# The two parts of the activations get a pool of their own, at a fixed distance from the weight parts

## The chip, the cores and the metric

One of the eight cores of a Trainium2 chip runs the whole program. The metric is the device time of one execution in microseconds, the median of three runs. TensorE (PE) multiplies, VectorE (DVE) and ScalarE (ACT) do everything between the products, SyncE (SP) issues the loads.

## The reference

A two-layer decoder trunk for 256 tokens of width 1024, in float32. Cut to what matters here:

```python
for l in range(DEPTH):                                   # two layers
    h = rmsnorm(x, norm_mix_g[l])
    if l % 2 == 0:
        proj = h @ e_w_in[e]                             # 1024 x 6144
        ya = rg_lru(causal_dwconv(xa), ...) * gelu(ga)
        yb = hgrn2_mix(qb, fb, ib, gb, ...)
        mix = concatenate([ya, yb]) @ e_w_out[e]         # 2048 x 1024
    else:
        proj = h @ o_w_in[o]                             # 1024 x 6176
        mix = mamba2_mix(...) @ o_w_out[o]               # 2048 x 1024
    x = x + mix
    x = x + mem_cross_attn(rmsnorm(x), rmsnorm(mem), xq_w[l], xk_w[l], xv_w[l], xo_w[l])
    hf = rmsnorm(x, norm_ffn_g[l])
    x = x + square(relu(hf @ ffn_w1[l])) @ ffn_w2[l]     # 1024 x 4096 x 1024
return rmsnorm(x, final_norm_g)
```

## The kernel before

All weights stream once from HBM, in an order fixed by `PLAN`, as halves of chunks of 128 x 1024 numbers. For each half SP loads a tile `raw` (line 150), ACT rounds it to float32r as `wh` (line 164), and DVE subtracts to give the rest as `wl` (line 165): two parts whose sum is the float32 weight. The class `Stream` keeps four `raw` buffers and five of each part, splits three halves ahead of the half being multiplied and loads four more ahead of that.

The activations are split in the same way, in tiles of 128 x 2 x 256 numbers (2048 bytes of a partition): `nh` and `nl` (helper `nhl`, four buffers each) after a norm, `yh` and `yl` (helper `yhl`, eight each) for the outputs of the mixers, the heads, the squared ReLU and the memory. A product of two split numbers is three matmuls, high by high, low by high and high by low. There are two kinds:

- `gemm` (lines 451, 453, 454): a 128 x 128 piece of `wh` or `wl` is loaded as the stationary matrix, and 256 columns of an activation part stream through as the moving one.
- `gemm_nat` (lines 470 to 472, and 1151 to 1153 at the very end): a 128 x 128 piece of an activation part is stationary, and 512 columns of weights move.

`chunk` issues them half by half, in the program's order, and between halves `pipe.tick()` lets the short chains of the norms, mixers and heads go on by one step. The scores and outputs of the heads (lines 804 to 806) are split products too, of scratch tiles; the mixers' small products are plain float32.

The tiles of SBUF lie in pools, one behind the other in the order in which these are opened: 16,512 bytes of what the system and its constants need, `cst` (small tables, the residual `xres`), `wp` (`raw`, `wh`, `wl`), `ap` (activations and scratch, each group of buffers behind the one first asked for), then `l0` or `l1`. Tiles are rounded up to 32 bytes. Adding up the sizes: every tile of `wp` begins 64 bytes beyond a multiple of 512, `yh` and `yl` begin 96 bytes beyond one, `nh` and `nl` 384 bytes beyond one. The pieces that matmuls take from them are at whole multiples of 512 bytes from there (`cs` of line 450 steps by 512 bytes, k by 1024), so each product meets the same remainders by 512.

Of the kernel before, what the change touches and what calls it, by code (L numbers as in the profile page):

```python
# [16 lines left out]
P = 128  # L17
# [7 lines left out]

# halves of weight chunks: buffers as loaded and as split, how far ahead they are split, and loaded before that
RAW_BUFS, PART_BUFS, SPLIT_AHEAD, LOAD_AHEAD = 4, 5, 3, 4
# chunks of layer 1's memory keys and values before the groups of the state-space mixer, and with each of them
KV_FIRST, *KV_EACH = 2, 2, 2, 2, 0, 0, 0, 0, 0
# how far short chains are taken ahead of the program's order  # L30
AHEAD = 200

# ---------------------------------------------------------------- the order of the weight chunks
# A chunk is 128 x (kt * cols) with kt * cols = 2048 (or less): kt k-tiles of a block of columns.

# [72 lines left out]

# ---------------------------------------------------------------- columns of the table of small parameters
_FIRST = [("memkv", 16), ("mix", 16)]  # L110
# [15 lines left out]
class Stream:  # L126
    """The halves of the weight chunks in their order: load, and split in two float32r parts."""

# [14 lines left out]
    def loading(self):  # L143
        """the next half, a piece at a time"""
        h = self.loaded
        self.loaded += 1
        hk, n = self._shape(h)
        self.raw[h] = raw = self.pool.tile([P, 1024], F32, tag="raw", bufs=RAW_BUFS, name=f"raw{h // 2}_{h % 2}")
        for a, b in self._pieces(h, hk * n):
            self.nc.sync.dma_start(raw[:, a:b], self.wst[h // 2, h % 2, :, a:b])  # L150
            yield
# [27 lines left out]
    def ahead(self, h):  # L179
        """what goes on while half h is multiplied"""  # L180
        with self.tc.high_priority(offset=0):
            self.split(h + 1 + SPLIT_AHEAD)
            self.load(h + 1 + SPLIT_AHEAD + LOAD_AHEAD)
# [7 lines left out]
class Pipe:  # L191
    """Chains of small steps that are issued a step at a time between the large products."""

# [19 lines left out]
def trunk(ctx: ExitStack, tc: tile.TileContext, wst, small, levels, gatew, xT, memT, fing, out):  # L213
# [3 lines left out]
    cst = ctx.enter_context(tc.tile_pool(name="cst", bufs=1))  # L217
    wp = ctx.enter_context(tc.tile_pool(name="wp", bufs=1))
    ap = ctx.enter_context(tc.tile_pool(name="ap", bufs=1))
    ps = ctx.enter_context(tc.tile_pool(name="ps", bufs=1, space=PSUM))  # L220
# [10 lines left out]
    def sc(i, name, shape=(P, 2, 256)):  # L231
        """scratch, two tiles of 2 KiB for each number"""
        return gt(name, f"s{i}", 2, shape)

    def nhl():
        return gt("nh", "nh", 4, dt=F32R), gt("nl", "nl", 4, dt=F32R)

    def yhl():
        return gt("yh", "yh", 8, dt=F32R), gt("yl", "yl", 8, dt=F32R)

# [29 lines left out]

    # ---------------------------------------------------------------- small helpers
    def seq():
        return tc.manual_schedule(engines={PE.engine})

    def order(after, before, why):
        """two instructions of one engine, in this order"""
        tc.add_manual_dep(after.ins, before.ins.name, NOSYNC, reason=why)
# [19 lines left out]
    def diag(r):  # L297
        """diagonal matrices of the two columns of r, in two parts"""
        dh, dl = (gt(t, t, 2, (P, 2, 128), F32R) for t in ("dgh", "dgl"))
        with tc.high_priority(offset=AHEAD):  # L300
            for j in range(2):
                V.tensor_scalar(dh[:, j, :], ident, r[:, j:j + 1], None, ALU.mult)
            for j in range(2):
                V.scalar_tensor_tensor(dl[:, j, :], ident, r[:, j:j + 1], dh[:, j, :].bitcast(F32),
                                       ALU.mult, ALU.subtract)
        return dh, dl
# [10 lines left out]
    def token_sums(sq, o, fold):  # L317
        """o[:, half] = the sum over channels of sq [channels, 2, tokens]"""
        n = 1 if fold else 2
        if fold:  # L320
            V.tensor_tensor(sq[:, 0, :], sq[:, 0, :], sq[:, 1, :], ALU.add)
        with seq():
            for hf in range(2):
                for c in range(n):
                    PE.matmul(o[:, hf:hf + 1], sq[:, c, 128 * hf:128 * hf + 128], ones[:, :1],  # L325
                              start=(c == 0), stop=(c == n - 1))
# [20 lines left out]
    def gained(hl, src, gain, i0):  # L347
        """src * gain (a column for each of the two tiles) in two parts"""
        h, lo = hl
# [6 lines left out]
    class Norm:  # L356
        """x * gain in two float32r parts, and 1 / rms of every token."""

# [18 lines left out]
        def add(s, xp, p, parts=True):  # L377
            """a chain of steps for one pair of tiles"""
            parts = parts and s.gain is not None
# [33 lines left out]
        def apply(s, xp, p):  # L413
            """the norm applied before the projection"""
            h = sc(3, "hx")
# [9 lines left out]

    # ---------------------------------------------------------------- products with the weights
    def chunk(label, piece, ticks=1, rows=1):
# [14 lines left out]
    def gemm(label, os, H, L, k0=0, first=True, last=True, ticks=1):  # L442
        """os[pair][:, j, :] += W[:, 128 columns of each]^T x over the k-tiles of a chunk"""
        kt = PLAN[st.pos][3]
# [19 lines left out]
    def gemm_nat(label, os, H, L, k0=0, first=True, last=True, ticks=1):  # L464
        """os[half] += x[tokens of the half]^T W over the k-tiles of a chunk, tokens on partitions"""
        kt = PLAN[st.pos][3]
# [8 lines left out]

    # ---------------------------------------------------------------- memory keys and values
    kT, vN = [[], []], [[], []]

    class Memory:
# [13 lines left out]
        def step(s, ticks=1):  # L493
            """the next chunk of the keys, then of the values"""
            i, l, n = s.done, s.l, s.n
# [76 lines left out]

    # ---------------------------------------------------------------- parameters of layer 0's mixers
    def pt():
# [33 lines left out]
    def conv(o, wn, bn, tiles, stride, cv):  # L608
        """width-4 causal depthwise convolution of two tiles"""
        r = sc(cv, "cv")  # L610
# [7 lines left out]

    # ---------------------------------------------------------------- RG-LRU
    def rglru(p, xc, ga):  # L620
# [33 lines left out]

    # ---------------------------------------------------------------- HGRN2
    sts = []
# [8 lines left out]
    def hgrn(p, F, K, q, Q, vg):  # L665
        """scores by halves of blocks of 2, 4, ... 256 tokens; every decay is a product of forget gates"""
        Qf, Kf, Tm = flat(Q), flat(K), flat(F)
# [114 lines left out]

    # ---------------------------------------------------------------- parts that both layers have
    def residual(o, p, nrm):
# [6 lines left out]
    def out_deep(label, H, L, nrm, ticks=1):  # L791
        """x += W^T y, 16 k-tiles in two sweeps over four accumulators"""
        os = [pg() for _ in range(4)]
# [6 lines left out]
    def products(o, pairs):  # L800
        """o = the sum of the products of (stationary, moving), each in two float32r parts"""
        last = len(pairs) - 1
# [5 lines left out]
    def parted(i, name, src):  # L808
        """two float32r parts of src"""
        h, lo = (gt(f"{name}{c}", f"s{i + c}", 2, dt=F32R) for c in range(2))  # L810
# [102 lines left out]

    # ---------------------------------------------------------------- layer 0
    pipe.drain()
# [12 lines left out]

    # ---------------------------------------------------------------- layer 1
    pipe.spawn(m1.prepare())  # L930
# [30 lines left out]
    def steps(o):  # L961
        """dt, and the sums of dt * A within each half of the tokens"""
        with tc.high_priority(offset=AHEAD):
# [30 lines left out]
    def decays(g):  # L994
        """exp(sum over s+1..t of dt A) of four heads, [s, (s0 t0 | s0 t1 | s1 t1)]"""
        E = l1.tile([P, 4, 3, 128], F32, tag="E", bufs=2, name=nm("E"))
# [27 lines left out]
    def ssd(g, E, xs, bc, z):  # L1024
        gap = 3 if g < 7 else 2
        for _ in range(gap):
            yield
        # masked C B^T, and x * dt with tokens on partitions
        cb = pm((P, 512))
# [83 lines left out]

    # ---------------------------------------------------------------- the last sum and norm, with tokens on partitions
    xn = [[sc(4 + 2 * hf + c, "xn", (P, 512)) for c in range(2)] for hf in range(2)]
# [3 lines left out]
    def turn():  # L1119
        """x with tokens on partitions, and the last gain for all of them"""  # L1120
        for c in range(2):
# [61 lines left out]

# ---------------------------------------------------------------- layout on the host

# [65 lines left out]
```

## Time and profile before

| what | value |
|---|---|
| device time, median of 3 runs | 1027.02 us (1026.95 to 1027.9) |
| span of the profiled execution, first to last instruction | 1024.7 us |
| TensorE busy, share of the span | 1012.2 us, 99% |
| VectorE busy | 773.8 us, 76% |
| ScalarE busy | 610.4 us, 60% |
| mean busy share of the DMA engines, and rate | about half, 176 GB/s |
| granted TensorE clock | 0.999 of full speed |

The profiled execution's time is known as its span; the runs are timed on the device as a whole and come out 2.3 us above it. "Busy" of TensorE counts a matmul from its start to its modelled end; consecutive matmuls overlap, so that the share says that TensorE always had one under way, and how fast they follow one another has to be read from their starts.

### The profile page before, as it was taken

What the parts mean: (1) busy time and instruction counts of PE and PEld (TensorE: products, weight loads), DVE (VectorE), ACT (ScalarE), POOL (GpSimd) and SP (SyncE); (2) the same over time, 40 slices, a digit from 0 to 9 for tenths busy, and PEclk for the clock granted to TensorE, in tenths of its full rate; (3) what the DMA queues carried; (4) which work ended last, traced back from release to release, by engine and by line L of the source; (5) the groups of instructions that cost most, each with busy time, mean ns of one, the idle gap of its engine ahead of it and who ended that gap; (6) DMA issues with size and microseconds to landing.
All of it is one profiled execution on the core that took longest, in us unless ns stands there. A gap on an engine that the chain in (4) does not pass through costs nothing.

```text
span 1024.7 us, 20857 instructions
## 1 busy us (share of the span) xinstructions
PE 1012.2 (99%) x8485; PEld 958.2 (94%) x8485; DVE 773.8 (76%) x1471; ACT 610.4 (60%) x886; POOL 1.2 (0%) x6
## 2 busy tenths in 40 slices
PE   8999999999999999999999999999999999999997
PEld 7898988989999999999999999999999999889985
DVE  7968788786887864565699888999989786546653
ACT  6667757674566653464546876778456656535542
POOL 0000000000000000000000000000000000000000
PEclk9999999999999999999999999999999999999999
DMA  8764443444544555555546665444545355555551
GB/s 292 273 218 157 140 150 135 175 146 146 183 145 166 185 185 185 186 187 187 173 150 219 217 189 202 169 162 144 206 135 195 129 166 181 185 185 185 187 184 41
DMA packets 52560, 180.54 MB, mean 176 GB/s; under 512 B 5968, under 2 KB 6128, under 8 KB 52336
## 3 DMA queue, kind: packets, MB, share of 16 engines
q1 hardware_dynamic: 52176, 178.69, 51.8%
q8 instruction: 66, 1.08, 0.4%
q10 hardware_dynamic: 288, 0.52, 0.1%
q14 instruction: 30, 0.25, 0.1%
HBM read 178.11 MB, written 1.08 MB: 175 GB/s over the span
## 4 chain that ended last, share of the span: by engine, by line
PE 90%; DVE 4%; ACT 4%; issue 1%; DMA 1%; SPq 0%; ACTq 0%
PE pg L451 23%; PE pg L453 22%; PE pg L454 22%; PE pg L472 4%; PE pg L470 4%; PE pg L471 4%; DVE wl L165 1%; ACT wh L164 1%; PE pm L325 1%; PE pm L1052 1%; PE pm L804 1%; PE pm L805 1%; PE pm L806 1%; DMA raw<-in_wst_dram 1%; PE pm L675 1%
## 5 line engine op out<-in xcount | busy, mean ns | idle before, releaser
L164 ACT CAST wh<-raw 128x1024 fp32r<-128x1024 f32 (+1 forms) x325 | 336.2, 1038 | 322.9 <-PE pg L453 219.9
L165 DVE TENSOR_TENSOR wl<-raw,wh 128x1024 fp32r<-128x1024 f32 (+1 forms) x325 | 391.4, 1209 | 164.6 <-ACT wh L164 163.9
L451 PE MATMUL pg<-nh,wh 128*128 128x256 f32 x1280 | 362.4, 283 | 0.0
L453 PE MATMUL pg<-nl,wh 128*128 128x256 f32 x1280 | 357.8, 280 | 0.0
L454 PE MATMUL pg<-nh,wl 128*128 128x256 f32 x1280 | 357.1, 279 | 0.0
L451 PEld LDWEIGHTS pg<-nh,wh 128*128 128x128 f32 x1280 | 240.5, 188 | 1.7 <-issue 0.7
L453 PEld LDWEIGHTS pg<-nl,wh 128*128 128x128 f32 x1280 | 240.1, 188 | 0.3
L454 PEld LDWEIGHTS pg<-nh,wl 128*128 128x128 f32 x1280 | 240.1, 188 | 0.0
L451 PE MATMUL pg<-yh,wh 128*128 128x256 f32 x768 | 215.4, 281 | 1.3 <-ACT yh L367 0.7
L453 PE MATMUL pg<-yl,wh 128*128 128x256 f32 x768 | 215.0, 280 | 0.1
L454 PE MATMUL pg<-yh,wl 128*128 128x256 f32 x768 | 214.7, 280 | 0.3 <-DVE wl L165 0.2
L451 PEld LDWEIGHTS pg<-yh,wh 128*128 128x128 f32 x768 | 144.3, 188 | 2.3 <-ACT wh L164 1.3
L454 PEld LDWEIGHTS pg<-yh,wl 128*128 128x128 f32 x768 | 144.2, 188 | 1.0 <-DVE wl L165 0.7
L453 PEld LDWEIGHTS pg<-yl,wh 128*128 128x128 f32 x768 | 144.3, 188 | 0.7 <-DVE yl L374 0.3
L470 PE MATMUL pg<-wh,yh 128*128 128x512 f32 x176 | 69.9, 397 | 0.0
L472 PE MATMUL pg<-wl,yh 128*128 128x512 f32 x176 | 69.6, 396 | 0.0
L471 PE MATMUL pg<-wh,yl 128*128 128x512 f32 x176 | 69.6, 395 | 0.0
L615 DVE SCALAR_TENSOR_TENSOR cv<-pg,smB,cv 128x255 f32<-128x255 f32 (+2 forms) x120 | 49.2, 473 | 0.5 <-ACT cv L612 0.5
L470 PEld LDWEIGHTS pg<-wh,yh 128*128 128x128 f32 x176 | 33.1, 188 | 7.9 <-issue 0.3
L472 PEld LDWEIGHTS pg<-wl,yh 128*128 128x128 f32 x176 | 33.1, 188 | 7.9
L471 PEld LDWEIGHTS pg<-wh,yl 128*128 128x128 f32 x176 | 33.1, 188 | 7.6
L896 DVE SCALAR_TENSOR_TENSOR t<-pg,rb 128x512 f32<-128x512 f32 x32 | 21.9, 690 | 16.5 <-PE pg L454 16.5
(262 smaller groups left out, 1097.5 us busy)
## 6 DMA issues: line engine op xcount, KB each, us to landing
raw<-in_wst_dram SPq DMA_DIRECT2D x317, 512.0 KB, 3.3
ac<-acd SPq DMA_DIRECT2D x16, 256.0 KB, 4.8
mem<-in_memT_dram SPq DMA_DIRECT2D x8, 256.0 KB, 4.4
raw<-in_wst_dram SPq DMA_DIRECT2D x8, 256.0 KB, 4.5
xres<-in_xT_dram SPq DMA_DIRECT2D x4, 256.0 KB, 6.4
gw<-in_gatew_dram SPq DMA_DIRECT2D x1, 1024.0 KB, 7.6
smB<-in_small_dram SPq DMA_DIRECT2D x1, 545.0 KB, 6.9
gn<-in_fing_dram SPq DMA_DIRECT2D x2, 256.0 KB, 3.8
```

The costliest lines, as they stand in the source:

```text
L164: self.last = nc.scalar.copy(hi[:, a:b], raw[:, a:b])
L165: nc.vector.tensor_tensor(lo[:, a:b], raw[:, a:b], hi[:, a:b].bitcast(F32), ALU.subtract)
L325: PE.matmul(o[:, hf:hf + 1], sq[:, c, 128 * hf:128 * hf + 128], ones[:, :1], start=(c == 0), stop=(c == n - 1))
L451: PE.matmul(o[:, j, :], wh[:, cs], xh, start=(first and k == 0 and j == 0), stop=False, skip_group_check=True)
L453: PE.matmul(o[:, j, :], wh[:, cs], xl, start=False, stop=False, skip_group_check=True)
L454: PE.matmul(o[:, j, :], wl[:, cs], xh, start=False, stop=(last and k == kt - 1), skip_group_check=True)
L470: PE.matmul(os[j], h, wh, start=(first and k == 0), stop=False)
L471: PE.matmul(os[j], lo, wh, start=False, stop=False)
L472: PE.matmul(os[j], h, wl, start=False, stop=(last and k == kt - 1))
L615: V.scalar_tensor_tensor(r[:, j, i:], o[:, j, :256 - i], col(wn, (3 - i) * stride + c), r[:, j, i:], ALU.mult, ALU.add)
L675: PE.matmul(tgt[32 * j:32 * j + 32, b // 4, :], Kf[:, 32 * b:32 * b + 32], qq[:, 32 * b:32 * b + 32], start=True, stop=True, tile_position ...
L896: V.scalar_tensor_tensor(t, o, 0.0, b2(n.rb), ALU.max, ALU.mult)
```

## The change

A new pool `mp` is opened between `wp` and `ap`. Its first tile, `shift`, is 112 float32 numbers (448 bytes of a partition) that nobody writes or reads. `nh`, `nl`, `yh` and `yl` now come from this pool with the same shapes, tags and numbers of buffers. Comments and docstrings go; nothing else differs.

```diff
+SHIFT = 112
...
     cst = ctx.enter_context(tc.tile_pool(name="cst", bufs=1))
     wp = ctx.enter_context(tc.tile_pool(name="wp", bufs=1))
+    mp = ctx.enter_context(tc.tile_pool(name="mp", bufs=1))
+    mp.tile([P, SHIFT], F32, name="shift")
     ap = ctx.enter_context(tc.tile_pool(name="ap", bufs=1))
...
+    def part(name, bufs):
+
+        return mp.tile([P, 2, 256], F32R, tag=name, bufs=bufs, name=nm(name))
+
     def nhl():
-        return gt("nh", "nh", 4, dt=F32R), gt("nl", "nl", 4, dt=F32R)
+        return part("nh", 4), part("nl", 4)
 
     def yhl():
-        return gt("yh", "yh", 8, dt=F32R), gt("yl", "yl", 8, dt=F32R)
+        return part("yh", 8), part("yl", 8)
```

By the sizes: `wp` still begins and ends 64 bytes beyond a multiple of 512 (its tiles are multiples of 4096), 448 bytes more make the remainder 0, and with tiles of 2048 bytes all of `nh`, `nl`, `yh`, `yl` begin at whole multiples of 512. The weights then lie 64 bytes beyond the activations, counted by 512, in every product of both kinds. Before, that distance was 480 for `yh` and `yl` (64 less 96) and 192 for `nh` and `nl` (64 less 384). What stays in `ap`, `l0` and `l1` moves back by 64 bytes, counted by 512.

## Rows read from the trace of the kernel before

**Rows 1.** The page: span, and each engine's busy time (share, instructions).

```profile
span 1024.7 us, 20857 instructions
PE 1012.2 (99%) x8485; PEld 958.2 (94%) x8485; DVE 773.8 (76%) x1471; ACT 610.4 (60%) x886; POOL 1.2 (0%) x6
```

**Rows 2.** The page: engines' shares of the chain that ended last.

```profile
PE 90%; DVE 4%; ACT 4%; issue 1%; DMA 1%; SPq 0%; ACTq 0%
```

**Rows 3.** The view of waits: who waited for whom, us in total, times, longest.

```profile
PE pm L523 <- DVE wz L520: 1.2, 1, 1.2
PE pm L675 <- DVE K L711: 1.0, 4, 0.3
...
ACT wh L164 <- PE pg L453: 219.9, 155, 3.4
```

**Rows 4.** Groups by line, TensorE: count after x, then busy us, mean ns.

```profile
L451 PE MATMUL pg<-nh,wh 128*128 128x256 f32 x1280 | 362.4, 283 | 0.0
...
L451 PE MATMUL pg<-yh,wh 128*128 128x256 f32 x768 | 215.4, 281 | 1.3 <-ACT yh L367 0.7 <-ACT wh L164 0.6
...
L470 PE MATMUL pg<-wh,yh 128*128 128x512 f32 x176 | 69.9, 397 | 0.0
...
L470 PE MATMUL pg<-wh,nh 128*128 128x512 f32 x64 | 26.0, 406 | 0.0
...
L804 PE MATMUL pm<-ph,kv 128*128 128x256 f32 x32 | 9.2, 288 | 0.0
...
L1151 PE MATMUL pg<-wh,yh 128*128 128x512 f32 x16 | 6.3, 396 | 0.0
```

**Rows 5.** TensorE by stretches: length, busy us (x matmuls under way in it), granted clock, DMA.

```profile
425.00:465.00 40.00, 40.00 (x342) 1.00 0.57 189
380.00:420.00 40.00, 40.00 (x345) 1.00 0.56 192
562.00:571.00 9.00, 9.00 (x81) 1.00 0.74 237
646.60:654.20 7.60, 7.60 (x69) 1.00 0.75 263
763.20:774.20 11.00, 11.00 (x96) 1.00 0.39 119
885.00:925.00 40.00, 40.00 (x173) 1.00 0.55 185
```

**Rows 6.** Timeline: first and last matmul of three of those stretches; start, duration, us.

```profile
424.81 0.28 PE L454 MATMUL pg<-nh,wl 128*128 128x256 f32 x1
464.98 0.28 PE L453 MATMUL pg<-nl,wh 128*128 128x256 f32 x1
379.77 0.28 PE L451 MATMUL pg<-yh,wh 128*128 128x256 f32 x1
419.90 0.28 PE L454 MATMUL pg<-yh,wl 128*128 128x256 f32 x1
561.82 0.28 PE L453 MATMUL pg<-nl,wh 128*128 128x256 f32 x1
570.89 0.28 PE L451 MATMUL pg<-nh,wh 128*128 128x256 f32 x1
```

**Rows 7.** Timeline: a matmul followed by a pause, between 96.1 and 96.5 us.

```profile
96.11 0.28 PE L453 MATMUL pg<-nl,wh 128*128 128x256 f32 x1
...
96.23 0.28 PE L454 MATMUL pg<-nh,wl 128*128 128x256 f32 x1
96.43 0.35 PEld L675 LDWEIGHTS pm<-Q,K 128*32 128x32 f32 x32
```

**Rows 8.** The chain in order of time: four plain float32 passes of 256 columns.

```profile
72.80 0.86 PE pm L624 x4
```

**Rows 9.** All engines in two stretches of 25 us: PE, PEld, DVE, ACT, POOL busy.

```profile
525.00:550.00 25.00, 24.51 (x204) 24.11 (x205) 24.83 (x47) 13.66 (x19) 0.00 (x0) 1.00 0.57 189
...
725.00:750.00 25.00, 25.00 (x220) 23.89 (x219) 24.40 (x62) 11.03 (x14) 0.00 (x0) 1.00 0.59 210
```

## Prediction before the run

> **What bounds the kernel now.** I read the page's busy times first. TensorE has a matmul under way in 99% of the span, VectorE 76%, ScalarE 60% [rows 1]. "Under way" is not "at its peak", so the chain that ended last comes next: 90% of it are TensorE's matmuls [rows 2]. Then the waits: the longest total wait of a TensorE matmul is 1.2 us, at the very start, and the next is 1.0 us in four pieces, while ScalarE's rounding of weights waits 219.9 us for TensorE to give buffers back [rows 3]. So the splitters and the loads are ahead, and the time is the number of products times the pace at which they follow each other. Nothing in the change alters the number; only the pace can move.
>
> The groups give the numbers [rows 4]. A line of a group stands for one of three matmuls of a split product, so: 3 x 1280 = 3840 products of 256 columns on `nh`/`nl`, 3 x 768 = 2304 on `yh`/`yl`, 3 x (176 + 64 + 16) = 768 of 512 columns with weights moving, and six kinds of 32 = 192 in the heads. Their mean durations (279 to 283 ns and about 396) are latencies and say nothing of the pace. The pace is the distance of starts in a steady stretch. From the first and last start and the count [rows 5, 6]:
>
> - `nh`/`nl`: (464.98 - 424.81) / 341 = 117.8 ns.
> - `yh`/`yl`: (419.90 - 379.77) / 344 = 116.7 ns. A later `yh` stretch has 96 in 11 us, (11.00 + 0.28) / 96 = 117.5 ns, within its resolution the 117.8 of the others.
> - 512 columns: (40.00 + 0.40) / 173 = 233.5 ns, twice that of 256 columns.
> - `nh`/`nl` again, at 562 to 571 us: (570.89 - 561.82) / 80 = 113.4 ns. The stretch at 646.6 to 654.2 us has (7.60 + 0.28) / 69 = 114.2 ns, the same within one product of its count. These are the same buffers as in the first line, at the same remainder by 512.
>
> The sum closes: 3690 x 117.8 + 150 x 113.4 + 2304 x 116.7 + 768 x 233.5 + 192 x 117.8 = 434.7 + 17.0 + 268.9 + 179.3 + 22.6 = 922 us, 90% of the span, as in the chain (150 is 81 + 69). The granted clock is 1.00 in all of these stretches [rows 5], so paces differ for another reason than the clock.
>
> How much room is there? Four passes of 256 columns of plain float32 take 0.86 us, 215 ns each [rows 8]; a split product has the 512-column matmul at 233.5 ns where this row takes 215. If a 256-column product could run at half of it, 107.5 ns, that would be its floor. I call this an estimate from rows 8. The products run 5% to 9% above the floor, and the fast stretch shows that some of that isn't fixed.
>
> **The change, part by part.** *The empty tile* has no instruction: no time. *The pool* has the same tags and buffer numbers, so no wait for a buffer is added and no instruction is moved past another; no DMA is touched. *Scratch* moves by 64 bytes: the heads' 192 products may change their pace by 4.4 ns (117.8 to 113.4), under 0.9 us either way; taken as 0. The plain float32 products I take as unchanged, since they go at the same pass time of 215 ns.
>
> *The remainders* are all that is left. Distance 192 (`nh`) and 480 (`yh`) become 64. No row shows 64, so the pace is bounded. From below: 107.5 ns, the floor. From above: the longest distance of two neighbouring starts that I can read in a steady stretch, 0.12 us [rows 7], so 120 ns for all. Between these I take 113.4 ns, the fastest pace that a row shows for this very sort of product. The reasons: the two groups differ by 1.1 ns at equal clock and equal shape, so layout does enter; `nh`, which begins at a multiple of 64, has reached 113.4, while no stretch of `yh`, which doesn't, is known to; and after the change every activation tile begins as evenly as `nh` and better. Against it: `nh` held 113.4 for only 150 of 3840 products, so even this layout chooses between two paces by how a stretch begins. That is why the chance below is under a half.
>
> - `nh`/`nl`: 3690 x (117.8 - 113.4) = 16.2 us.
> - `yh`/`yl`: 2304 x (116.7 - 113.4) = 7.6 us.
> - 512 columns: weights still move, from the same remainder 64; what was loaded beside them lay at 96 or 384 and comes to lie at 0. Taken as 0; if it followed (233.5 to 226.9, the ratio of 113.4 to 116.7) it would give 768 x 6.6 = 5.1 us more.
>
> What comes late next is VectorE. Twenty-five microseconds at the new pace become 25 x 113.4 / 117.8 = 24.07, and VectorE has 24.83 and 24.40 us of work in the two fullest such stretches [rows 9]: 0.8 + 0.3 = 1.1 us come back. Elsewhere its waits for ScalarE and TensorE are slack.
>
> Sum: 1024.7 - 16.2 - 7.6 + 1.1 = 1002.0 us of span. The median of the runs, 1027.0, is 2.3 us above the profiled span, which I add: 1004.3 us.
>
> [...] A matmul with no weight load beside it shows whether loads and moving reads disturb each other. At 96.23 us a product starts, the next load begins 0.20 us later, when its columns have passed, and yet it takes 0.28 us like the one before it, which had a load beside it [rows 7]; ends are modelled, so this is a hint and no proof. [...]
>
> **The rivals.**
>
> 1. *The change does nothing for the pace.* The stall is the moving stream's own, whatever lies beside it: for it the row at 96.23 us, and that one layout has two paces. Against it the steady 1.1 ns between `nh` and `yh`. Time 1027.0.
> 2. *A small gain:* all 256-column products settle at 116.7 ns, the pace of `yh`. -3690 x 1.1 + 150 x 3.3 = -3.6 us: 1023.4.
> 3. *A small loss, the other side:* with everything aligned like `nh`, everything takes `nh`'s usual pace, 117.8 ns. `yh` loses 2304 x 1.1 = 2.5 us, the fast stretches 150 x 4.4 = 0.7: 1030.2. It decides wherever a stretch fails to fall into the fast pace; `nh` fails in 96% of its products.
> 4. *A larger loss:* at a distance of 64 the moving read, twice as fast, catches up with the weight read just after each start and is held back every time. All at 120 ns: 3690 x 2.2 + 150 x 6.6 + 2304 x 3.3 = 16.7 us: 1043.7. Single distances of 0.12 us speak for it, the steady means of 116.7 to 117.8 against.
> 5. *No stall at all:* 107.5 ns for 256 columns, 3690 x 10.3 + 150 x 5.9 + 2304 x 9.2 = 60.1 us, and with 215 for 512 columns 768 x 18.5 = 14.2 more. VectorE's two stretches give back 25 x 107.5 / 117.8 = 22.8, so 2.0 + 1.6 = 3.6 us. 970.5 without the 512-column part, 956.3 with it.
>
> **How the numbers follow.** The forecast 0.38, rival 1 0.18, 2 0.12, 3 0.15, 4 0.10, 5 0.07. What can be told from no change is 0.2%, 2 us. Faster: 0.38 + 0.12 + 0.07 = 0.57; same: 0.18; slower: 0.15 + 0.10 = 0.25. The range: rivals 1 to 3 and the forecast hold 0.83. Its low end is a pace half way to the floor, 110.45 ns: 3690 x 7.35 + 150 x 2.95 + 2304 x 6.25 = 42.0 us, with 2.4 us back for VectorE 987, and 5.1 less if the 512-column products follow: 982. Its high end is rival 3 with another 0.6 ns on 6144 products: 1034. The forecast's own range, with the same low end and its paces between 110.45 and 114.2, is 982 to 1009.
>
> **What would show it.** In the profile after, the stretches at the same work should have starts 113 to 114 ns apart for both `nh` and `yh`, with no third pace: that is the step that carries 23.8 us. The 512-column stretches should stay at 233.5. Counts of matmuls must be the same, and TensorE's waits a few us at most; VectorE's share rises to 78%. If `nh` stays at 117.8 and `yh` moves towards it, rival 3 is right; if both keep their paces, rival 1. I am wrong outright if the pace goes by how a stretch begins and not by the layout: then no layout holds a fast pace, and the fast stretches only move elsewhere.

## The result and the profile after

| | before | after |
|---|---|---|
| device time, median of 4 runs each | 1027.09 us (1026.95 to 1027.9) | 1010.22 us (1009.63 to 1016.65) |
| ratio | 1 | 0.9849, 95% interval 0.9831 to 0.9868 |
| span of the profiled execution | 1024.7 us | 1008.5 us |
| forecast | | 1004.3 us, range 982 to 1034 |

The change makes the kernel 1.5% faster, 16.9 us, against a forecast of 22.7. The instructions are the same on every engine, in the same order; only line numbers move (the three matmuls of a 256-column split product are now L459, L461 and L462, those of 512 columns L478 to L480).

The page of the changed kernel: span, busy times (share, instructions), shares of the chain that ended last. They answer to [rows 1, 2].

```profile
span 1008.5 us, 20857 instructions
...
PE 994.4 (99%) x8485; PEld 943.2 (94%) x8485; DVE 773.4 (77%) x1471; ACT 610.6 (61%) x886; POOL 1.2 (0%) x6
...
PE 84%; DVE 8%; ACT 4%; issue 1%; DMA 1%; SPq 0%; ACTq 0%
```

TensorE's busy time falls by 17.8 us and the span by 16.2; the work of the other engines is what it was. VectorE's part of the chain doubles from 4% to 8%: of the other engines it grows most. The waits of the changed kernel, against [rows 3] (us in total, times, longest):

```profile
PE pm L683 <- DVE K L719: 1.4, 4, 0.5
PE pm L531 <- DVE wz L528: 1.2, 1, 1.2
...
ACT wh L166 <- PE pg L461: 206.1, 154, 3.4
```

TensorE still waits for almost nothing, so the gain must lie in the pace. TensorE by stretches of one sort of product, against [rows 5] (length, busy us, x matmuls under way, granted clock, DMA share and GB/s):

```profile
245.00:265.00 20.00, 20.00 (x172) 1.00 0.55 187
383.00:415.00 32.00, 32.00 (x285) 1.00 0.57 196
430.00:460.00 30.00, 30.00 (x267) 1.00 0.58 196
526.00:538.00 12.00, 12.00 (x108) 1.00 0.83 254
872.00:912.00 40.00, 40.00 (x176) 1.00 0.58 189
```

By the prediction's rule, (length + one product) / count: `yh` at 383 us goes at (32 + 0.28) / 285 = 113.3 ns (before 116.7), `nh` at 430 us at 30.28 / 267 = 113.4 (before 117.8), `nh` at 526 us at 12.28 / 108 = 113.7, within one product of the same. The 512-column products at 872 us go at 40.39 / 176 = 229.5; first and last start of their 192, 869.98 and 913.69 us, give the better 43.71 / 191 = 228.9 (before, in the same way, 882.81 to 927.36: 233.2). But the first row is `yh` as well, at the same layout and clock, and goes at 20.28 / 172 = 117.9 ns, slower than before. So the changed kernel has two paces.

Over the whole program I take the starts in the trace. In undisturbed stretches of 20 and more there are 5637 products of 256 columns: 4163 of them (74%) follow each other at 113.3 ns, 1474 at 117.8, and the 116.7 of `yh` is gone. Apart from its first few distances, no stretch of them changes its pace before something interrupts it.

The balance of the span, each matmul counted from its start to the next one's: `nh` of 256 columns -11.2 us, `yh` of 256 columns -5.1, 512 columns -2.9; pauses of over 135 ns (260 for 512 columns) +2.9 (`yh` 1.7, `nh` 0.8, 512 columns 0.4); all else +0.1. Together -16.2, the difference of the spans.

### The profile page after: what moved, and what is told of

It is laid out like the page before. It is cut to its first block, busy times and chain, and to the rows that moved or that the text cites. A ratio compares the mean times of both kernels' runs of the same rounds, so it can differ in the third digit from the quotient of the medians.

```text
span 1008.5 us, 20857 instructions
## 1 busy us (share of the span) xinstructions
PE 994.4 (99%) x8485; PEld 943.2 (94%) x8485; DVE 773.4 (77%) x1471; ACT 610.6 (61%) x886; POOL 1.2 (0%) x6
## 4 chain that ended last, share of the span: by engine, by line
PE 84%; DVE 8%; ACT 4%; issue 1%; DMA 1%; SPq 0%; ACTq 0%
PE pg L459 21%; PE pg L461 20%; PE pg L462 20%; PE pg L480 4%; PE pg L479 4%; PE pg L478 4%; DVE wl L167 3%; ACT wh L166 1%; PE pm L333 1%; PE pm L812 1%; PE pm L1060 1%; PE pm L813 1%; PE pm L814 1%; DVE cv L623 1%; PE pm L683 1%
## 5 line engine op out<-in xcount | busy, mean ns | idle before, releaser
L459 PE MATMUL pg<-nh,wh 128*128 128x256 f32 x1280 | 360.1, 281 | 0.0
L461 PE MATMUL pg<-nl,wh 128*128 128x256 f32 x1280 | 355.5, 278 | 0.0
L462 PE MATMUL pg<-nh,wl 128*128 128x256 f32 x1280 | 355.3, 278 | 0.0
L459 PEld LDWEIGHTS pg<-nh,wh 128*128 128x128 f32 x1280 | 240.5, 188 | 1.7 <-issue 0.7
L461 PEld LDWEIGHTS pg<-nl,wh 128*128 128x128 f32 x1280 | 241.2, 188 | 0.3
L462 PEld LDWEIGHTS pg<-nh,wl 128*128 128x128 f32 x1280 | 240.9, 188 | 0.0
L459 PE MATMUL pg<-yh,wh 128*128 128x256 f32 x768 | 214.4, 280 | 1.0 <-ACT wh L166 1.0
L461 PE MATMUL pg<-yl,wh 128*128 128x256 f32 x768 | 213.8, 279 | 0.3 <-DVE yl L382 0.2
L462 PE MATMUL pg<-yh,wl 128*128 128x256 f32 x768 | 213.5, 279 | 0.4 <-DVE wl L167 0.2
L459 PEld LDWEIGHTS pg<-yh,wh 128*128 128x128 f32 x768 | 144.4, 188 | 1.9 <-ACT wh L166 1.4
L462 PEld LDWEIGHTS pg<-yh,wl 128*128 128x128 f32 x768 | 144.4, 188 | 1.1 <-DVE wl L167 0.8
L461 PEld LDWEIGHTS pg<-yl,wh 128*128 128x128 f32 x768 | 144.3, 188 | 1.2 <-DVE yl L382 0.9
L480 PE MATMUL pg<-wl,yh 128*128 128x512 f32 x176 | 69.3, 394 | 0.0
L478 PE MATMUL pg<-wh,yh 128*128 128x512 f32 x176 | 68.7, 391 | 0.0
L478 PEld LDWEIGHTS pg<-wh,yh 128*128 128x128 f32 x176 | 33.0, 188 | 7.4 <-issue 0.3
L480 PEld LDWEIGHTS pg<-wl,yh 128*128 128x128 f32 x176 | 33.1, 188 | 6.7
```

The lines of the kernel that those rows point to most:

```text
L459: PE.matmul(o[:, j, :], wh[:, cs], xh, start=(first and k == 0 and j == 0), stop=False, skip_group_check=True)
L461: PE.matmul(o[:, j, :], wh[:, cs], xl, start=False, stop=False, skip_group_check=True)
L462: PE.matmul(o[:, j, :], wl[:, cs], xh, start=False, stop=(last and k == kt - 1), skip_group_check=True)
L478: PE.matmul(os[j], h, wh, start=(first and k == 0), stop=False)
L480: PE.matmul(os[j], h, wl, start=False, stop=(last and k == kt - 1))
```

## The experiments

**Other distances.** Is it the distance between what is loaded and what moves that sets the pace, is it the activations' own alignment, or neither? In these seven kernels `nh`/`nl` and `yh`/`yl` have a pool each, and pads in front of them choose the distances separately; the pad behind them puts scratch at its remainder of the changed kernel. The exceptions are the kernel with everything moved up, where scratch moves along, and the last one, which puts it where it was before the change. All distances are counted by 512, as weights less activations. The common edit, against the changed kernel, with the pads' sizes in bytes as `p1`, `p2`, `p3` (a pad of size 0 is left out):

```diff
-    mp = ctx.enter_context(tc.tile_pool(name="mp", bufs=1))
-    mp.tile([P, SHIFT], F32, name="shift")
+    pad(tc.tile_pool(name="pad1", bufs=1), p1)
+    mn = ctx.enter_context(tc.tile_pool(name="mn", bufs=1))
+    pad(tc.tile_pool(name="pad2", bufs=1), p2)
+    my = ctx.enter_context(tc.tile_pool(name="my", bufs=1))
+    pad(tc.tile_pool(name="pad3", bufs=1), p3)
...
-        return mp.tile([P, 2, 256], F32R, tag=name, bufs=bufs, name=nm(name))
+        pool = mn if name[0] == "n" else my
+        return pool.tile([P, 2, 256], F32R, tag=name, bufs=bufs, name=nm(name))
```

*Distance 0 for `nh`, 128 for `yh`:*

```diff
+p1, p2, p3 = 0, 384, 64
```

> Weights lie 0 bytes beyond nh/nl and 128 beyond yh/yl (by 512); nothing else differs from the changed kernel. Theory D (the pace goes by the distance between what is loaded and what moves): the paces of nh and yh differ from each other and from the 113.3/117.8 mix, and 512-column products on yh leave 228.9 ns. Theory A (it goes by the alignment of the moving tile alone, multiples of 64 are equal): the same two paces 113.3 and 117.8 in both groups, 512 columns at 228.9, 1008 to 1015 us. Theory S (only by how a stretch begins): two paces in other shares, 1005 to 1028 us.

1038.58 us, ratio 1.0113 (1.0083 to 1.0142). Stretches of `yh`, `nh` and 512 columns on `yh`:

```profile
383.00:415.00 32.00, 32.00 (x269) 1.00 0.55 183
430.00:460.00 30.00, 30.00 (x252) 1.00 0.55 181
896.00:936.00 40.00, 40.00 (x174) 1.00 0.55 188
```

32.28 / 269 = 120.0 and 30.28 / 252 = 120.2 ns: slower than either pace of before, though both sorts of tile begin at multiples of 64 bytes. That rules out Theory A.

*Distance 256 for `nh`, 320 for `yh`:*

```diff
+p1, p2, p3 = 256, 448, 256
```

> Weights 256 bytes beyond nh/nl and 320 beyond yh/yl. Theory D: paces of their own, at least one other than 113.3 and 117.8; distances far from 64 no better than the 116.7 to 117.8 of the kernel before, so 1020 to 1035 us. Theory A: as the changed kernel, 1008 to 1015 us. Theory S: two paces in other shares, 1005 to 1028 us.

1027.64 us, ratio 1.0009 (0.9997 to 1.002). The same three stretches:

```profile
383.00:415.00 32.00, 32.00 (x285) 1.00 0.59 194
430.00:460.00 30.00, 30.00 (x253) 1.00 0.56 184
886.00:926.00 40.00, 40.00 (x177) 1.00 0.57 188
```

`yh` at 113.3 ns and `nh` at 119.7 beside each other in one program. 320 gives the pace of 64 (113.3) and 256 that of 0 (120.0 in both by the map below): the distance counts by 256, not by 512. That distances far from 64 would be no better than before, as expected, is wrong for 320. The gain of `yh` and the loss of `nh` cancel in the total.

*Distance 384 for `nh`, 448 for `yh`:*

```diff
+p1, p2, p3 = 128, 448, 384
```

> Weights 384 bytes beyond nh/nl and 448 beyond yh/yl. Theory D: paces of their own; 448 is the mirror of 64 (weights 64 bytes before), and 480 had 116.7 steadily, so 1015 to 1035 us. Theory A: as the changed kernel, 1008 to 1015 us. Theory S: two paces in other shares, 1005 to 1028 us.

1032.82 us, ratio 1.0056 (1.0033 to 1.0079). `yh`, then `nh`:

```profile
383.00:415.00 32.00, 32.00 (x274) 1.00 0.52 182
430.00:460.00 30.00, 30.00 (x255) 1.00 0.55 186
```

117.8 and 118.7 ns. The first is the pace that `nh` had in the kernel before, at the same distance by 256; that 448 might mirror 64 does not come true.

*All moved up by 64 bytes, the distance left at 64:*

```diff
+    pad(tc.tile_pool(name="pad0", bufs=1), 64)
     wp = ctx.enter_context(tc.tile_pool(name="wp", bufs=1))
...
+p1, p2, p3 = 448, 0, 0
```

> The changed kernel with everything from the weights on moved up by 64 bytes: the distance stays 64, the weights begin at 128 and the activations at 64. Theory D: as the changed kernel, paces 113.3 and 117.8, 512 columns at 228.9, 1008 to 1015 us. Theory A with an alignment of 128 or more: yh and nh leave these paces; with an alignment of 64 it stays. Theory S: the stretches that are fast change places, 1005 to 1028 us.

1013.27 us, ratio 0.9866 (0.9838 to 0.9895). `yh`, `nh`, the `nh` stretch that went at 113.7 ns in the changed kernel, 512 columns:

```profile
383.00:415.00 32.00, 32.00 (x285) 1.00 0.57 193
430.00:460.00 30.00, 30.00 (x267) 1.00 0.59 194
527.00:540.00 13.00, 13.00 (x113) 1.00 0.80 257
874.00:914.00 40.00, 40.00 (x177) 1.00 0.57 193
```

The same two paces (113.3 and 113.4 ns in the first two rows), and 228.9 ns for 512 columns from the first and last start. The remainders themselves leave these as they are; the distance sets them. The third row is at 13.28 / 113 = 117.5 ns: 14 stretches have the other pace than in the changed kernel, and fewer products are fast (3827 of 5655), some 340 by 4.45 ns or 1.5 of the 3 us between the two; part of the rest are longer pauses. So the layout decides which paces there are, and something else which of the two a stretch takes. The layout also weighs the two: `nh` before, at 192, had the same pair, 113.4 and 117.8, but only 4% of its products in the two fast stretches that the prediction read, against 74% here at 64.

*Distance 32 for `nh`, 96 for `yh`, and 160 and 224:*

```diff
+p1, p2, p3 = 480, 448, 32     # 32 and 96
...
+p1, p2, p3 = 352, 448, 160    # 160 and 224
```

> Weights 32 bytes beyond nh/nl, 96 beyond yh/yl: both sides of 64. The runs so far: 0 and 256 bytes pace at 119.8 ns, 64 and 320 at 113.3 or 117.8, 128 and 384 at 118.5 to 119, 192 and 448 at 117.8. Theory P (the pace goes by the distance by 256, smoothly, with its best near 64): nh between 113.3 and 119.8 and yh between 113.3 and 119, 1008 to 1030 us. Theory 64 (reads go in pieces of 64 bytes, and a distance that is no multiple of 64 behaves as the kernel before's 480): 116.7 in both, about 1023 us.

> Weights 160 bytes beyond nh/nl, 224 beyond yh/yl. 224 is 480 by 256. Theory P (period 256): yh paces at 116.7 as in the kernel before, its 512-column products at 233.3, and nh, at a distance not tried, between 117.8 and 119; 1025 to 1033 us. Theory W (the whole distance by 512 counts): yh at another pace than 116.7.

1031.8 us, ratio 1.0043 (1.0023 to 1.0062), and 1035.43 us, ratio 1.0081 (1.0052 to 1.011). `yh` and `nh` of the first:

```profile
383.00:415.00 32.00, 32.00 (x276) 1.00 0.53 182
430.00:460.00 30.00, 30.00 (x256) 1.00 0.55 184
```

and of the second:

```profile
383.00:415.00 32.00, 32.00 (x277) 1.00 0.55 185
430.00:460.00 30.00, 30.00 (x253) 1.00 0.59 188
```

Neither reaches 113.3. The first settles its two theories: 118.4 and 117.3 (by the map below) are not the 116.7 of Theory 64, and Theory P has its range of paces right, but not its time (1030 us at most), and the map is not smooth around one best place: 224 is faster than 192 and 0 on either side of it. In the second `nh` goes at 30.28 / 253 = 119.7, not at the 117.8 to 119 that were expected, and the time is 2 us above the expected range. The second's `yh`, 32.28 / 277 = 116.5, has the pace of `yh` before, where the distance was 480: again the same by 256.

*Only `nh` and `nl` moved, `yh`, `yl` and scratch at the remainders of before:*

```diff
+p1, p2, p3 = 448, 96, 480
```

> One part of the change alone: nh/nl at distance 64, yh/yl left at 480 and the scratch at its remainders of before. nh should take 113.3 or 117.8 as in the changed kernel, yh 116.7 as before: of the changed kernel's 16.2 us the nh part is 10.4 (11.1 less 0.8 of longer waits), so 1016 to 1018 us. If the two groups' gains depend on each other, or the move of the scratch carries part of it, it is off this by more than 2 us.

1017.94 us, ratio 0.9911 (0.9882 to 0.994). `yh`, `nh`, 512 columns on `yh`:

```profile
383.00:415.00 32.00, 32.00 (x276) 1.00 0.56 185
430.00:460.00 30.00, 30.00 (x267) 1.00 0.58 194
878.00:918.00 40.00, 40.00 (x173) 1.00 0.56 185
```

`yh` stays at 32.28 / 276 = 117.0 and 512 columns at 40.39 / 173 = 233.5, `nh` drops to 113.4. That is 9.2 us of the changed kernel's 16.9; the rest is what `yh` brings, its 512-column products included.

The map, from the first and last start of the same 384 products in each trace, divided by 383 (`nh` before: 423.51 and 468.62 us), and for 512 columns of the same 192 on `yh`, divided by 191:

| distance by 256 | `nh`, ns | `yh`, ns | 512 columns on `yh`, ns |
|---|---|---|---|
| 0 | 120.0 (at 0 and at 256) | | |
| 32 | 118.4 | | |
| 64 | 113.3 (also with everything 64 higher) | 113.3; 113.4 at 320 | 228.9 (at 64 and at 320) |
| 96 | | 117.3 | 233.4 |
| 128 | 118.6 | 120.0, a later stretch 118.7 | 232.4 |
| 160 | 120.0 | | |
| 192 | 117.8 (before) | 117.8 | 233.3 |
| 224 | | 116.7 (before, and at 224) | 233.3 |

The 512-column products on `nh` come in four stretches of 23 or 24 only. The third of them goes at (170.70 - 165.57) / 22 = 233.2 ns before, at 192; (168.31 - 163.27) / 22 = 229.1 at 64; and (171.56 - 166.53) / 22 = 228.6 at 0, a distance at which 256 columns are slowest; past its first eight products that one goes at (171.56 - 168.61) / 13 = 226.9. So the two shapes don't want the same distance, and 64 is near the best for both.

**What picks the pace of a stretch?** Two kernels put one plain float32 product of `ident` ahead of the first chunk of each accumulator outside the memory's keys, 104 in all; what it writes is overwritten. The layout is that of the changed kernel. If the entry of a stretch decides, the length of this product must shift the paces; if chance or another engine's traffic does, it should not do so in a regular way.

```diff
+        if first and label[:2] != "k0":
+            with seq():
+                PE.matmul(os[0][0:32, 1, 224:256], ident[:, 0:32], ident[:, 0:32], start=True, stop=True,
+                          tile_position=(0, 0), skip_group_check=True)
...
+                PE.matmul(os[0][:, 1, 128:256], ident, ident, start=True, stop=True, skip_group_check=True)
         chunk(label, piece, ticks, len(os))
```

The first form, of 32 columns:

> The changed kernel with one plain float32 matmul of 32 columns (its result is overwritten) ahead of the first chunk of each accumulator, 104 in all. In the changed kernel a stretch never changes its pace once under way, and all 18 stretches that follow 32-to-128-column passes of Q and K are fast. Theory E (how a stretch is entered decides its pace): the stretches behind these matmuls, entered all alike, have nearly all one pace, more than 90% of their products, likely 113.3 ns. Theory R (the pace is drawn anew, or set by what goes on elsewhere): about 7 in 10 products fast as before. Time: 104 breaks of 0.1 to 0.25 us, so 1015 to 1035 us in either case.

The second, of 128 columns:

> The same with a matmul of 128 columns on a 128 x 128 matrix, as in a transposition: 5 of 7 stretches behind the transpositions of xs are slow in the changed kernel, and both behind those of the heads. Theory E: nearly all stretches behind it have one pace, and not that of the run with 32 columns: 117.8 ns. Theory R: shares as in the changed kernel. Time 104 breaks of 0.15 to 0.3 us, and 10 to 20 us more if the pace is 117.8: 1025 to 1055 us.

1041.47 us, ratio 1.0142 (1.0122 to 1.0162), and 1037.49 us, ratio 1.0103 (1.0083 to 1.0123). As a change both only cost: the 104 products add 27 to 31 us to the changed kernel's time, the first more than the expected 1035 us at most. What they tell lies in the timeline (start, duration, us; the trace has two records for each extra product, and the first is shown). Four of the 32-column products in a row, with 48 products of `nh` behind each:

```profile
346.24 0.22 PE L467 MATMUL pg<-smB 128*32 128x32 f32 x1
352.06 0.22 PE L467 MATMUL pg<-smB 128*32 128x32 f32 x1
357.89 0.22 PE L467 MATMUL pg<-smB 128*32 128x32 f32 x1
363.73 0.22 PE L467 MATMUL pg<-smB 128*32 128x32 f32 x1
```

5.82 to 5.84 us apart, three times alike. The same four of 128 columns, and the next:

```profile
346.80 0.27 PE L467 MATMUL pg<-smB 128*128 128x128 f32 x1
352.68 0.27 PE L467 MATMUL pg<-smB 128*128 128x128 f32 x1
358.36 0.27 PE L467 MATMUL pg<-smB 128*128 128x128 f32 x1
364.24 0.27 PE L467 MATMUL pg<-smB 128*128 128x128 f32 x1
369.92 0.27 PE L467 MATMUL pg<-smB 128*128 128x128 f32 x1
```

5.88, 5.68, 5.88, 5.68 us: strictly in turn. 0.20 us over the 47 distances behind each is 4.3 ns, the gap between the two paces. The entry of the first and of the second of these stretches:

```profile
346.94 0.36 PE L459 MATMUL pg<-nh,wh 128*128 128x256 f32 x1
347.14 0.28 PE L461 MATMUL pg<-nl,wh 128*128 128x256 f32 x1
347.26 0.28 PE L462 MATMUL pg<-nh,wl 128*128 128x256 f32 x1
347.38 0.28 PE L459 MATMUL pg<-nh,wh 128*128 128x256 f32 x1
...
352.82 0.37 PE L459 MATMUL pg<-nh,wh 128*128 128x256 f32 x1
353.03 0.28 PE L461 MATMUL pg<-nl,wh 128*128 128x256 f32 x1
353.15 0.28 PE L462 MATMUL pg<-nh,wl 128*128 128x256 f32 x1
353.26 0.28 PE L459 MATMUL pg<-nh,wh 128*128 128x256 f32 x1
```

The first distance is 0.20 us in the one (201 ns in the trace) and 0.21 in the other (207); the third is 0.12 and 0.11. What lies ahead of the entry alternates as well: the two records of the extra product are 108 ns apart ahead of the slow stretches and 114 ahead of the fast ones, so that each stretch seems to hand the next one the other entry. Over the whole program, 24 of 26 stretches behind 108 ns are slow, and 26 of 26 behind 113 or 114 fast. These same products all went at 113.4 ns in the changed kernel without the extra product. Of the undisturbed stretches of 20 and more behind an extra product, 77 of 91 are fast with 32 columns and 47 of 90 with 128. By products 83% and 60% are fast, where Theory E had over 90% at one pace and Theory R about 70% as in the changed kernel: neither came true as written. That the longer one would make all stretches slow did not come true either: it makes every second one slow. That the entry decides is supported all the same: by an edit at the entry alone, stretches take the other pace to their end, and the work of ScalarE and VectorE does not alternate with them. ScalarE begins to round weights 0.08 us behind the extra product at 364.24 us, which has a fast stretch behind it, and 0.09 us behind the one at 369.92, which has a slow one:

```profile
364.32 1.05 ACT L166 CAST wh<-raw 128x1024 fp32r<-128x1024 f32 x1 [1.77 <-PE pg L461]
370.01 1.05 ACT L166 CAST wh<-raw 128x1024 fp32r<-128x1024 f32 x1 [1.67 <-PE pg L461]
```

VectorE's next work begins 0.20 us behind either. Of all undisturbed stretches of the 128-column kernel, the 35 that begin with a first distance of 206 or 207 ns are all fast; of the 66 with 200 to 202, 20 are. The number is not a threshold: in the changed kernel 20 of 20 behind 222 to 224 ns are fast and 4 of 4 behind 305 slow.

The 512-column products have two paces at distance 64 as well, which only this kernel shows at length. Of its two runs of 192 on `yh`, the first and the second:

```profile
895.00:935.00 40.00, 40.00 (x173) 1.00 0.58 191
985.00:1025.00 40.00, 40.00 (x177) 1.00 0.36 119
```

From first and last start they go at (937.98 - 893.41) / 191 = 233.4 and (1028.16 - 984.45) / 191 = 228.9 ns; in the changed kernel both go at 228.9.

**Is the pattern chance?** The changed kernel, unaltered:

> The changed kernel once more, unaltered: 1009 to 1017 us. Theory E with an entry that varies from run to run: its times spread more than those of the kernel before (which has nearly one pace for each tile group), and some stretches, not most, have the other pace than in the first profile. If the pace is fixed by the program, the same stretches are fast.

1010.81 us, ratio 0.9839 (0.9823 to 0.9856). The stretches shown of the changed kernel, in the new trace:

```profile
383.00:415.00 32.00, 32.00 (x285) 1.00 0.60 196
430.00:460.00 30.00, 30.00 (x267) 1.00 0.59 196
245.00:265.00 20.00, 20.00 (x173) 1.00 0.57 186
526.00:538.00 12.00, 12.00 (x109) 1.00 0.83 259
872.00:912.00 40.00, 40.00 (x176) 1.00 0.61 194
```

Counts equal within one. Of some 80 stretches two have the other pace than in the first trace: mostly the program sets the pattern.

## Why the prediction was right, and where it missed

*The bound and the step that carries the gain* were right: TensorE's matmuls follow each other at a pace that the layout sets (113.3 to 120.0 ns over the distances tried), at a granted clock of 1.00 throughout, and at distance 64 both `nh` and `yh` reach the 113.4 ns taken from one fast stretch of before. The argument for it was wrong, though. It leaned on every activation tile beginning at a multiple of 64 or more; the kernel moved up by 64 bytes keeps the pace with other remainders, and the kernel with `nh` at distance 0 has tiles as even and runs at 120.0. What counts is the distance, by 256 (113.3 and 113.4 ns at 64 and 320, 120.0 at 0 and 256). That 64 is the one distance, of the eight tried, at which most products go at 113.3 was no part of the argument: there the forecast was lucky.

*The term that was mis-sized:* "all 256-column products at 113.4". 74% get there and the others go at 117.8, which for `yh` is slower than before. It was booked as -16.2 and -7.6 us and came out as -11.2 and -5.1: 7.5 us short. The doubt was in the text (a layout that "chooses between two paces by how a stretch begins") but only as a chance, not as a share of the products. Half of the closing sentence, "the pace goes by how a stretch begins and not by the layout", is what happens, only that it is both: the layout sets which paces there are and how often the fast one is taken (4% of `nh` in the two stretches read at 192, 74% of the products at 64), and by the extra products the entry picks (83% fast behind the 32 columns, 60% behind the 128).

*The 512-column products*, taken as 0, went from 233.3 to 228.9 ns on `yh`: 2.9 us gained, where the text had allowed 5.1.

*What VectorE gives back* was 1.1 us by two stretches; pauses grew by 2.9 in all. I did not trace each of them to VectorE. The heads' 192 products, put down at 117.8 ns in the sum, go at 120.0 before and 120.1 after; the 0 taken for their change was right.

With these, 1002.0 + 7.5 - 2.9 + 1.8 = 1008.4, the measured span within 0.1. The runs stand 1.7 us above the profiled span where 2.3 had been added.

*Rival 1* (the stall is the moving stream's own) is out: with the same instructions, moving only the activations took the same 384 `nh` products from 113.3 to 120.0 ns. In the 512-column products the moving tile is the weights' and stayed where it was; only what is loaded moved, and the pace went from 233.3 to 228.9. These two measurements show that for split float32r products the distance between what is loaded and what moves does count. The row at 96.23 us, taken as a hint that loads and moving reads do not disturb each other [rows 7], showed modelled ends (0.28 us with a load beside it and without), and was no evidence. *Rivals 2 and 3* would have left 116.7 or 117.8 everywhere: 116.7 occurs nowhere now, 117.8 in a quarter. *Rival 4*, 120 ns, exists, but at distances 0, 128 and 160; that a moving read twice as fast catches up with the weight read no trace shows. *Rival 5*, no stall at all, occurs at no distance tried (113.3 ns is the fastest for 256 columns, where it asked for 107.5); plain float32 passes cost what they did (from start to start, 65.3 us for all of them before and 65.4 after).

**What stays open.** How the two reads meet inside TensorE no trace shows: the map is a measurement, not a mechanism. Steps finer than 32 bytes were not tried. How the entry picks the pace is not known either: the first distance goes with it, but that it is the cause is not shown, and 14 stretches behind the 32-column product are slow although all are entered by the same instruction. Nor is it known why `yh` took the fast pace in 91% of its products at 320 and in 73% at 64, which are the same distance by 256. One of the eight runs of the changed kernel took 1016.65 us. The 1440 products from 341.3 to 504.4 us are one unbroken fast stretch; at the slow pace they would add 1440 x 4.45 = 6.4 us, which is just that run's distance to the median. That run has no trace, so this is an argument and not shown.

## What to carry to other kernels

When an engine is busy 99% of the time and waits for nothing, read the distance of starts in long undisturbed stretches, one for each pair of operand tiles: two numbers for the same shape at the same clock (117.8 and 116.7 ns before) were here a sign that the layout costs something, and a pad that has no instruction was worth 1.5%. Try the distance of loaded and moving operand over one whole period (here 256 bytes in steps of 32: the best, 64, at 113.3 ns and the worst, 0 and 160, at 120.0 differ by 6%) and not one value, since the neighbours of the good distance were no better than the rest (118.4 at 32, 117.3 at 96). Where a trace shows two paces under one layout, forecast with a share of the products and not with all or none; and a total that doesn't move (1.0009 here) can hold a gain and a loss of the same size (`yh` from 116.7 to 113.3 ns, `nh` from 117.8 to 120.0).

## What was not expected of the hardware

- The pace of split products depends on the distance between the loaded and the moving tile by 256 bytes: 113.3 to 120.0 ns for 256 columns, 226.9 (once settled, at 0) to 233.4 for 512, at a granted clock of 1.00; distance 0 is among the slowest for 256 columns and the fastest for 512.
- At distance 64 two paces, 113.3 and 117.8 ns, exist side by side. A stretch keeps the one it began with, the longest for 1440 products in a row. Both paces occur at little and at much DMA work: 117.9 at a DMA share of 0.55 and 117.5 at 0.80, 113.3 at 0.57 and 113.7 at 0.83.
- Six nanoseconds at the entry (201 or 207 ns to the second product, behind the 128-column product) go with 0.20 us in the next 48, and a slow stretch is followed by a fast one and that by a slow one.
